# Two transformer blocks on one core: where the second block's modulation products run

## The chip, the cores and the metric

One NeuronCore of a Trainium2 chip runs the whole program. The metric is the device time of one execution in microseconds (us); the median of a few executions counts. TensorE (PE) multiplies matrices, VectorE (DVE), ScalarE (ACT) and GpSimd (POOL) work element by element, and SP does nothing here but issue transfers (DMA).

## What is computed

A first block mixes a sequence of 256 tokens, 1024 wide, with a diagonal state space model; a second model of two layers follows, whose norms and gates are modulated by a condition vector. Cut to what the change touches:

```python
def first_block(x, ...):                       # DEPTH = 1
    h = rmsnorm(x, norm_mix)
    x = x + s5_mixer(h, ...)                   # state space, then a * sigmoid(g), [a, g] = gelu(y) @ w_glu
    x = x + sqrelu_mlp(rmsnorm(x, norm_ffn), mlp_w1, mlp_w2)
    x = x + (p @ ple_w) * sigmoid(rmsnorm(x, norm_ple) @ ple_gate_w)
    return rmsnorm(x, norm_final)

def second_block(x, c, ctx, c_ctx, w_ada, b_ada, ...):
    for l in range(2):
        mod_x = silu(c) @ w_ada[l] + b_ada[l]      # (1, 6144): shift, scale, gate, twice
        mod_c = silu(c_ctx) @ w_ada[l] + b_ada[l]
        ...                                        # hx = modulate(rms_norm(x), ...), four mixers, swiglu
```

The modulation products are `silu(c) @ w_ada[l]` for two vectors at once: two columns against a matrix of 1024 x 6144 in float32, 25 MB of weights per layer. All of it is read once.

## The kernel before, in words

Activations lie features on partitions, 256 tokens along the free axis. Layer weights come by `wunits` (lines 340 to 351) in units of 128 x 1024: a transfer by SP, a cast on ACT to the high part `wh`, a subtraction on VectorE to the low part `wl`. `mm3` (353 to 365) then makes three matmuls for each 128 x 128 piece: high by high, high by low, low by high.

**Stages.** `s5` (655 to 808) is the state space stage. `s5_params` (496 to 596) computes decay powers on VectorE in many small operations. For eight groups of states `b_outer` makes outer products, which TensorE transposes and multiplies with the input (699 to 725). Then `c_outer` makes the output side (732 to 737) and `s5_scan` runs the scan on VectorE. TensorE forms Toeplitz blocks `kt` (742 to 757), which 32 transfers per run, 16 for each half, scatter into `mt` (759 to 763; the last of them on SP is kept as `m_dma`), and two sets of products with `mt` (780) and with the scanned states `zf` (792) give the output. `ple_proj` (826) loads and multiplies the side input; it is put behind `m_dma` on that transfer's queue (1707). `block1` (841) is the gated unit over eight output tiles (847 to 860) and the feed-forward stage in four parts (868 to 901). The second block's layers follow: `mixer`, `ffn` (1572).

**Modulation products, first layer.** `ada_steps(g)` (951 to 967), for three groups g of 2048 columns, is a generator. Each of 16 steps takes a chunk of 128 x 1024 (0.5 MB, one SP transfer into a stage buffer) and makes four products of 256 columns into the four 32-partition column groups of one PSUM tile; the stationary side is the activated condition vector `sc` (`silu_c`, 940). A float32 product stands in the trace as two matmuls. Two more steps copy the sums out and turn them by four transposes (`ada_turn`, 969). In `s5` the stage buffers are the three of pool `wa` (1688); after `s5` they are the three buffers `k4a`.

**Modulation products, second layer.** `ada_late` (977 to 1004) goes over 12 blocks of 512 columns. VectorE multiplies each chunk's rows by the condition's value and adds them up (lines 992 and 994, four operations a step, four steps a block), and TensorE adds the 128 partitions up with a stationary matrix of ones: two products of 512 columns a block, one per vector (998). Every second block is turned.

**Order.** The calls `ada_next(n)` (1010) pull n steps at a place in the program; after `s5_params` 4, then 2 for each of eight groups on the input side and 2 for each of eight on the output side, 2 for each output tile of the gated unit, 1 for each of eight units of the first two feed-forward parts. A planner orders each engine's instructions from their place in the program, their inputs and its own estimate of times; steps of the modulation inside `s5` get a place 50 instructions later (`ADA_OFF`). The order on each engine and each queue is fixed before the run, and each engine takes its list strictly in that order. `issue_after(ins)` puts what is made inside it behind `ins` on that engine's list, without a wait of its own.

Of the kernel before, what the change touches and what calls it, by code (L numbers as in the profile page):

```python
# [17 lines left out]
P = 128  # L18
# [260 lines left out]
class Net:  # L279
    def __init__(self, tc, aps, dbg=None):  # L280
        self.tc, self.nc, self.a, self.dbg = tc, tc.nc, aps, dbg or {}
        nc = self.nc
        self.V, self.S, self.G, self.T = nc.vector, nc.scalar, nc.gpsimd, nc.tensor
        self.n = 0
        self.ln = "m"


# [65 lines left out]
    def mm3(self, out, unit, act, ks, off=0, start=True, stop=True, cols=None):  # L353

        wh, wl = unit
        n = len(ks)
        for i, k in enumerate(ks):
            c = off + i * P
# [296 lines left out]
    def s5(self):  # L655
# [6 lines left out]
        with self.lane("a"):  # L662
            dm = self.k2([P, 16, 2, 16], F32, "dm")
        G.tensor_tensor(dm.rearrange("p a b c -> p a (b c)"), self.eye2.unsqueeze(1).to_broadcast([P, 16, 32]),
                        par("d").unsqueeze(2).to_broadcast([P, 16, 32]), op=ALU.mult)
        self.s5_params()
        self.silu_c()

# [3 lines left out]
        for h in range(2):  # L672
# [8 lines left out]
            u2.append(u)  # L681
        self.ada_next(4)
        y = self.rstd(pss, 32, 1.0 / D, EPS)
# [15 lines left out]
        for jp in range(4):  # L699
            ss_sb = self.k4([P, 2, 2, 2, 64], F32, "ss")  # L700
            for jj in range(2):
                pt = self.q4.tile([P, 4, 2, 8, 16], F32, tag="pt", name=self.nm("pt"))
                self.b_outer(pt, (jp * 2 + jj) * 4, bre, bim)
                self.ada_next(2)
                pmt = self.k4([P, 4, 2, P], F32, "pmt")
# [26 lines left out]
        for j in range(8):  # L732
            c = self.k4([P, 8, 8, 16], F32, "ca")
            for g0 in (0, 4):
                self.c_outer(c[:, g0 : g0 + 4], j * 8 + g0, c1, c2)
            self.ada_next(2)
            ca[j] = c
# [4 lines left out]
        for half in range(2):  # L742
# [16 lines left out]
            for i in range(16):  # L759
                r4, g4 = i // 4, i % 4  # L760
                dma = (G if half and i % 3 == 2 else nc.sync).dma_start(
                    mt[half][32 * r4 : 32 * r4 + 32, g4, :, 0 : P - 32 * r4],
                    kt[half][32 * g4 : 32 * g4 + 32, :, 32 * r4 : P])
                if half and i % 3 < 2:
                    self.m_dma = dma
# [6 lines left out]
        pss = {}  # L772
# [68 lines left out]
    def block1(self, ya, pe, early, fill):  # L841
# [5 lines left out]
        for f in range(KC):  # L847
# [9 lines left out]
            self.ssq_add(ssq, x[:, f], f, KC)  # L857
            self.ada_next(2)
            if f == 4:
# [8 lines left out]
        for part in range(4):  # L868
            ma = Act(self, KC, L, "m")
            for c in range(4):  # L870
# [7 lines left out]
                self.split(*ma.pair(c * 2), s)  # L878
                if part < 2:
                    self.ada_next()  # L880
                if part >= 1:
# [95 lines left out]
    def ada_late(self):  # L977


        V, S, T = self.V, self.S, self.T  # L980
        for b in range(12):
            if b % 2 == 0:
                ps = self.px([P, 512])
            acc = self.stage([P, 2, 512], F32, "ac")
            for k in range(0, KC, 2):
                st = self.stage([P, 2, 512], F32, "wa")
                self.nc.sync.dma_start(st.rearrange("p a b -> p (a b)"), self.a["w_ada1"][b * 4 + k // 2])
                for i in range(2):
                    for v in range(2):
# [3 lines left out]
                        else:  # L993
                            V.scalar_tensor_tensor(acc[:, v], st[:, i], c, acc[:, v], op0=ALU.mult, op1=ALU.add)  # L994
                yield
            for v in range(2):
                r = 64 * (b % 2) + 32 * v
                T.matmul(ps[r : r + 32, :], self.ones[:, 0:32], acc[:, v], start=True, stop=True)
            if b % 2:
                pt = self.ada_turn(ps).rearrange("p i (q s) c -> p i q s c", s=2)  # L1000
                for q in range(2):
                    c0 = (b - 1 + q) * 4
                    S.copy(self.mod[1][:, c0 : c0 + 4, :], pt[:, :, q, :, 0])
                yield

# [636 lines left out]
    def run(self):  # L1642
        tc, nc = self.tc, self.nc
        V, S, G = self.V, self.S, self.G
        with ExitStack() as st:
# [19 lines left out]
            with ExitStack() as s5s:  # L1665
# [21 lines left out]
                nc.sync.dma_start(self.s5v[:, 1200:], self.a["s5"][:, 1200:])  # L1687
                self.stage = lambda shape, dt, s: self.wa.tile(shape, dt, tag="wa", name=self.nm(s))
                self.ada_off = ADA_OFF
# [130 lines left out]
```

## Time and profile before

| | us |
|---|---|
| median of 3 runs | 1978.75 (1974.57 to 1979.27) |
| profiled execution | 1979.86 |
| its span, first to last instruction | 1978.1 |
| TensorE busy | 1890.7 (96%) |
| VectorE busy | 1525.5 (77%) |
| ScalarE busy | 932.4 (47%) |

Times in rows are counted from the span's start. Busy time says how long an engine had an instruction under way; neighbouring matmuls overlap, so the distance from one start to the next tells what a matmul costs in a row of them. The share of one engine in the chain of waits tells how much of the span it decided.

### The profile page before, as it was taken

To read this page: it belongs to the slowest core of one execution; us is meant where nothing else is said; L and a number is where in the kernel's file an instruction comes from. 1 tells how busy PE (TensorE), PEld (TensorE's weight loads), DVE (VectorE), ACT (ScalarE), POOL (GpSimd) and SP (SyncE) were. 2 spreads that over 40 slices of the span, in tenths; PEclk is the share of its full clock that TensorE was granted. 3 is DMA by queue.
4 is the path that set the end of the run, shared out by engine and by line. 5 is a ranking of instruction groups with operands and counts; after the bars stand their busy time and mean duration, and the time that the engine had idled before them with its cause. 6 is when DMAs were issued, how large, how long until landed. Compare 5 with 4: busy or idle time off the path is not lost.

```text
span 1978.1 us, 35512 instructions
## 1 busy us (share of the span) xinstructions
PE 1890.7 (96%) x13842; PEld 1676.3 (85%) x13842; DVE 1525.5 (77%) x3078; ACT 932.4 (47%) x1587; POOL 112.1 (6%) x130
## 2 busy tenths in 40 slices
PE   2879999999999999999999999999999999999997
PEld 1567899998799997799998777777997799989997
DVE  9853777799987789998788577665779997776665
ACT  2453545555655555654553222222556664544443
POOL 5410100000000011000000000000100000010000
PEclk9989999999999999999999999999999999999998
DMA  5686556664345654246555455453555235555663
GB/s 183 223 264 225 183 181 196 192 181 142 98 138 170 200 181 158 62 127 206 175 181 159 124 170 150 152 167 112 146 171 160 71 107 172 180 181 163 191 191 107
DMA packets 103192, 323.45 MB, mean 164 GB/s; under 512 B 16416, under 2 KB 18608, under 8 KB 102640
## 3 DMA queue, kind: packets, MB, share of 16 engines
q1 hardware_dynamic: 102256, 319.53, 52.1%
q8 instruction: 109, 1.79, 0.4%
q0 software_dynamic: 336, 1.44, 0.2%
q14 instruction: 59, 0.48, 0.1%
q10 hardware_dynamic: 432, 0.21, 0.0%
HBM read 317.47 MB, written 1.05 MB: 161 GB/s over the span
## 4 chain that ended last, share of the span: by engine, by line
PE 79%; DVE 12%; DMA 4%; ACT 2%; issue 2%; SPq 1%; POOL 0%; DVEq 0%; ACTq 0%; POOLq 0%
PE pm L363 19%; PE pm L364 19%; PE pm L365 18%; DVE wl L332 4%; PE pm L1071 3%; PE pm L1072 3%; PE pm L1073 3%; DVE cy L1102 2%; DMA wa<-w_ada 2%; PE px L960 2%; PE px L1393 2%; PE px L1342 1%; PE px L1375 1%; PE px L404 1%; ACT wh L331 1%
## 5 line engine op out<-in xcount | busy, mean ns | idle before, releaser
L331 ACT CAST wh<-ws 128x1024 fp32r<-128x1024 f32 (+3 forms) x556 | 533.1, 961 | 713.3 <-PE pm L364 403.6
L332 DVE TENSOR_TENSOR wl<-ws,wh 128x1024 fp32r<-128x1024 f32 (+3 forms) x556 | 616.1, 1116 | 270.7 <-ACT wh L331 267.7
L363 PE MATMUL pm<-h,wh 128*128 128x256 f32 (+1 forms) x928 | 297.8, 321 | 0.0
L364 PE MATMUL pm<-h,wh 128*128 128x256 f32 (+1 forms) x928 | 297.2, 320 | 0.0
L365 PE MATMUL pm<-h,wl 128*128 128x256 f32 (+1 forms) x928 | 296.8, 320 | 0.0
L363 PE MATMUL pm<-m,wh 128*128 128x256 f32 (+1 forms) x704 | 211.6, 301 | 0.0
L364 PE MATMUL pm<-m,wh 128*128 128x256 f32 (+1 forms) x704 | 211.2, 300 | 0.0
L365 PE MATMUL pm<-m,wl 128*128 128x256 f32 (+1 forms) x704 | 210.6, 300 | 0.0
L363 PEld LDWEIGHTS pm<-h,wh 128*128 128x128 f32 x928 | 174.6, 188 | 18.5 <-ACT wh L331 4.2
L364 PEld LDWEIGHTS pm<-h,wh 128*128 128x128 f32 x928 | 174.8, 188 | 14.6 <-issue 0.8
L365 PEld LDWEIGHTS pm<-h,wl 128*128 128x128 f32 x928 | 174.6, 188 | 14.4
L363 PE MATMUL pm<-hx,wh 128*128 128x256 f32 x640 | 183.3, 286 | 0.0
L364 PE MATMUL pm<-hx,wh 128*128 128x256 f32 x640 | 179.9, 281 | 0.0
L365 PE MATMUL pm<-hx,wl 128*128 128x256 f32 x640 | 179.6, 281 | 0.0
L1102 DVE SCALAR_TENSOR_TENSOR cy<-up,vecs,cy 128x256 f32<-128x256 f32 x360 | 161.9, 480 | 1.4
L363 PEld LDWEIGHTS pm<-m,wh 128*128 128x128 f32 x704 | 132.2, 188 | 9.3 <-ACT wh L331 1.7
L994 DVE SCALAR_TENSOR_TENSOR ac<-wa,sc,ac 128x512 f32<-128x512 f32 x168 | 117.8, 749 | 28.8 <-DMA wa<-w_ada 28.8
L364 PEld LDWEIGHTS pm<-m,wh 128*128 128x128 f32 x704 | 132.6, 188 | 7.5 <-issue 1.7
L365 PEld LDWEIGHTS pm<-m,wl 128*128 128x128 f32 x704 | 132.5, 188 | 5.7
L429 POOL TENSOR_TENSOR ssq<-ssq,sq 128x256 f32<-128x256 f32 x45 | 44.9, 999 | 1425.9 <-ACT sq L423 1424.4
L363 PEld LDWEIGHTS pm<-hx,wh 128*128 128x128 f32 x640 | 121.0, 189 | 2.2 <-issue 2.0
L365 PEld LDWEIGHTS pm<-hx,wl 128*128 128x128 f32 x640 | 121.0, 189 | 0.0
(444 smaller groups left out, 4224.0 us busy)
## 6 DMA issues: line engine op xcount, KB each, us to landing
wa<-w_ada SPq DMA_DIRECT2D x96, 512.0 KB, 4.1
ws<-w_gp SPq DMA_DIRECT2D x96, 512.0 KB, 3.6
ws<-w_f SPq DMA_DIRECT2D x88, 512.0 KB, 4.4
ws<-w_tok SPq DMA_DIRECT2D x76, 512.0 KB, 3.8
ws<-mlp_w SPq DMA_DIRECT2D x64, 512.0 KB, 4.2
ws<-w_gp SPq DMA_DIRECT2D x96, 256.0 KB, 2.7
ws<-w_f2a SPq DMA_DIRECT2D x32, 512.0 KB, 4.1
ws<-w_cin SPq DMA_DIRECT2D x24, 512.0 KB, 4.5
```

Of the source, the lines that this page charges most:

```text
L331: self.S.copy(hi, src)
L332: self.V.tensor_tensor(lo, src, hi.bitcast(F32), op=ALU.subtract)
L363: self.T.matmul(out, h, ah, start=start and i == 0, stop=False)
L364: self.T.matmul(out, h, al, start=False, stop=False)
L365: self.pe_last = self.T.matmul(out, l, ah, start=False, stop=stop and i == n - 1)
L429: (eng or self.G).tensor_tensor(acc, acc, sq, op=ALU.add)
L960: T.matmul(ps[32 * q : 32 * q + 32, hf * 256 : hf * 256 + 256], self.sc[:, k, :], st[:, q, :], start=k == 0, stop=k == KC - 1)
L994: V.scalar_tensor_tensor(acc[:, v], st[:, i], c, acc[:, v], op0=ALU.mult, op1=ALU.add)
L1071: self.T.matmul(ps, hi, a, start=k == 0, stop=False)
L1072: self.T.matmul(ps, lo, a, start=False, stop=False)
L1073: self.pe_last = self.T.matmul(ps, hi, b, start=False, stop=k == KC - 1)
L1102: V.scalar_tensor_tensor(y[:, k], up[:, k, i : i + L], w[:, i : i + 1], y[:, k], op0=ALU.mult, op1=ALU.add)
```

## The change

All 54 steps of the first layer's modulation are pulled inside `s5`: 6 ahead of `s5_params` (with the activation of the condition vector ahead of those), 3 in place of 2 for each group on the input and on the output side. The calls in the gated unit and in the first block's feed-forward stage go. Of the first 30 stage buffers two in five are halves of the residual `x`, which is loaded only later; so five are in turn instead of three. Of the second half's 16 scatter transfers, the 11 that SP issued are issued by ACT, so `m_dma` is ACT's. In the second layer a block's sums are made one step later than its last addition, as four products of 256 columns in four column groups, and the next `mm3` is put behind the last of them. All steps of the second layer then run in the first layer's `ffn`, 49 of them.

```diff
--- before.py
+++ after.py
@@ -283,6 +283,7 @@
         self.V, self.S, self.G, self.T = nc.vector, nc.scalar, nc.gpsimd, nc.tensor
         self.n = 0
         self.ln = "m"
+        self.ada_last = None
 
 
     def nm(self, s):
@@ -352,6 +353,10 @@
 
     def mm3(self, out, unit, act, ks, off=0, start=True, stop=True, cols=None):
 
+        if self.ada_last is not None:
+            was, self.ada_last = self.ada_last, None
+            with self.tc.issue_after(was.ins):
+                return self.mm3(out, unit, act, ks, off, start, stop, cols)
         wh, wl = unit
         n = len(ks)
         for i, k in enumerate(ks):
@@ -663,8 +668,9 @@
             dm = self.k2([P, 16, 2, 16], F32, "dm")
         G.tensor_tensor(dm.rearrange("p a b c -> p a (b c)"), self.eye2.unsqueeze(1).to_broadcast([P, 16, 32]),
                         par("d").unsqueeze(2).to_broadcast([P, 16, 32]), op=ALU.mult)
+        self.silu_c()
+        self.ada_next(6)
         self.s5_params()
-        self.silu_c()
 
         sh = [P, 32, 32]
         u2 = []
@@ -679,7 +685,6 @@
             u = self.k4(sh, F32, "u2")
             G.tensor_tensor(u, x2, par("gain")[:, h * 32 : h * 32 + 32].unsqueeze(2).to_broadcast(sh), op=ALU.mult)
             u2.append(u)
-        self.ada_next(4)
         y = self.rstd(pss, 32, 1.0 / D, EPS)
         for h in range(2):
             V.tensor_tensor(u2[h], u2[h], y.unsqueeze(1).to_broadcast(sh), op=ALU.mult)
@@ -701,7 +706,7 @@
             for jj in range(2):
                 pt = self.q4.tile([P, 4, 2, 8, 16], F32, tag="pt", name=self.nm("pt"))
                 self.b_outer(pt, (jp * 2 + jj) * 4, bre, bim)
-                self.ada_next(2)
+                self.ada_next(3)
                 pmt = self.k4([P, 4, 2, P], F32, "pmt")
                 for g2 in range(2):
                     ps = self.pm([P, 4, P])
@@ -733,7 +738,7 @@
             c = self.k4([P, 8, 8, 16], F32, "ca")
             for g0 in (0, 4):
                 self.c_outer(c[:, g0 : g0 + 4], j * 8 + g0, c1, c2)
-            self.ada_next(2)
+            self.ada_next(3)
             ca[j] = c
 
         zf = self.s5_scan(zb)
@@ -758,7 +763,7 @@
 
             for i in range(16):
                 r4, g4 = i // 4, i % 4
-                dma = (G if half and i % 3 == 2 else nc.sync).dma_start(
+                dma = (nc.scalar if half and i % 3 < 2 else G if half else nc.sync).dma_start(
                     mt[half][32 * r4 : 32 * r4 + 32, g4, :, 0 : P - 32 * r4],
                     kt[half][32 * g4 : 32 * g4 + 32, :, 32 * r4 : P])
                 if half and i % 3 < 2:
@@ -855,7 +860,6 @@
             V.scalar_tensor_tensor(x[:, f], s, 0.5, x[:, f], op0=ALU.mult, op1=ALU.add)
             self.split_scaled(ha.hi(f), ha.lo(f), x[:, f], self.vec("norm_ffn", f))
             self.ssq_add(ssq, x[:, f], f, KC)
-            self.ada_next(2)
             if f == 4:
                 nc.sync.dma_start(self.cx.rearrange("p a b -> p (a b)"), self.a["cT"])
         r2 = self.k1([P, L], F32, "r2")
@@ -876,8 +880,6 @@
                 S.activation(s, ps, AF.Relu)
                 V.tensor_tensor(s, s, s, op=ALU.mult)
                 self.split(*ma.pair(c * 2), s)
-                if part < 2:
-                    self.ada_next()
                 if part >= 1:
                     next(early, None)
             for c in range(4):
@@ -977,10 +979,26 @@
     def ada_late(self):
 
 
+
         V, S, T = self.V, self.S, self.T
+        pss = []
+
+        def products(b, acc):
+            if b % 2 == 0:
+                pss.append(self.px([P, 512]))
+            ps = pss[-1]
+            for q in range(2):
+                for v in range(2):
+                    r = 64 * q + 32 * v
+                    self.ada_last = T.matmul(ps[r : r + 32, b % 2 * 256 : b % 2 * 256 + 256], self.ones[:, 0:32],
+                                             acc[:, v, q * 256 : q * 256 + 256], start=True, stop=True)
+            if b % 2:
+                pt = self.ada_turn(ps).rearrange("p (b i) (q s) c -> p b q i s c", b=2, s=2)
+                for i in range(2):
+                    c0 = (b - 1 + i) * 4
+                    S.copy(self.mod[1][:, c0 : c0 + 4, :].rearrange("p (q i) s -> p q i s", i=2), pt[:, i, :, :, :, 0])
+
         for b in range(12):
-            if b % 2 == 0:
-                ps = self.px([P, 512])
             acc = self.stage([P, 2, 512], F32, "ac")
             for k in range(0, KC, 2):
                 st = self.stage([P, 2, 512], F32, "wa")
@@ -992,16 +1010,12 @@
                             V.tensor_scalar(acc[:, v], st[:, i], c, None, op0=ALU.mult)
                         else:
                             V.scalar_tensor_tensor(acc[:, v], st[:, i], c, acc[:, v], op0=ALU.mult, op1=ALU.add)
+                if k == 0 and b:
+                    products(b - 1, was)
                 yield
-            for v in range(2):
-                r = 64 * (b % 2) + 32 * v
-                T.matmul(ps[r : r + 32, :], self.ones[:, 0:32], acc[:, v], start=True, stop=True)
-            if b % 2:
-                pt = self.ada_turn(ps).rearrange("p i (q s) c -> p i q s c", s=2)
-                for q in range(2):
-                    c0 = (b - 1 + q) * 4
-                    S.copy(self.mod[1][:, c0 : c0 + 4, :], pt[:, :, q, :, 0])
-                yield
+            was = acc
+        products(11, was)
+        yield
 
     def ada_bias(self, l):
         b = self.vec("b_ada", l * 48, 48).unsqueeze(2).to_broadcast([P, 48, 2])
@@ -1685,7 +1699,16 @@
                 for h in range(2):
                     nc.sync.dma_start(self.x2[h].rearrange("p g c -> p (g c)"), self.a["x2"][:, h * 1024 : h * 1024 + 1024])
                 nc.sync.dma_start(self.s5v[:, 1200:], self.a["s5"][:, 1200:])
-                self.stage = lambda shape, dt, s: self.wa.tile(shape, dt, tag="wa", name=self.nm(s))
+                stages = iter(range(99))
+
+                def stage(shape, dt, s):
+                    i = next(stages)
+
+                    if i < 30 and i % 5 > 2:
+                        return self.x[:, i % 5 * 4 - 12 : i % 5 * 4 - 8]
+                    return self.wa.tile(shape, dt, tag="wa", name=self.nm(s))
+
+                self.stage = stage
                 self.ada_off = ADA_OFF
                 self.todo = chain(*(self.ada_steps(g) for g in range(3)))
                 ya = self.s5()
```

## Rows read from the trace of the kernel before

**Rows 1.** Chain that ended last, share of the span by engine.

```profile
PE 79%; DVE 12%; DMA 4%; ACT 2%; issue 2%; SPq 1%; POOL 0%; DVEq 0%; ACTq 0%; POOLq 0%
```

**Rows 2.** Windows by stage: stretch, length, busy per engine (instructions), clock, DMA share, GB/s.

```profile
4.00:17.00 13.00, 0.00 (x0) 0.00 (x0) 12.55 (x56) 0.41 (x2) 6.19 (x4) 1.00 0.86 326
17.00:32.00 15.00, 1.51 (x4) 0.63 (x4) 14.96 (x53) 5.31 (x11) 7.04 (x5) 1.00 0.00 0
32.00:74.00 42.00, 36.21 (x358) 18.68 (x359) 33.91 (x59) 20.65 (x43) 22.43 (x23) 0.96 0.63 205
74.00:104.00 30.00, 21.91 (x480) 13.58 (x484) 28.49 (x64) 11.68 (x36) 11.17 (x10) 0.94 0.87 255
104.00:123.00 19.00, 12.77 (x271) 10.82 (x269) 9.43 (x13) 6.32 (x7) 6.66 (x18) 0.73 0.77 182
135.60:209.79 74.19, 74.19 (x523) 53.67 (x521) 29.78 (x39) 26.57 (x41) 3.67 (x5) 1.00 0.72 243
213.00:241.00 28.00, 25.68 (x218) 24.88 (x218) 26.05 (x59) 17.30 (x31) 6.30 (x5) 1.00 0.61 182
1020.00:1410.00 390.00, 389.03 (x1868) 311.65 (x1866) 266.53 (x417) 114.59 (x169) 9.57 (x10) 1.00 0.48 148
```

**Rows 3.** Timeline of TensorE, gated-unit stage: start, us, engine, line, operation, out and in.

```profile
135.61 0.28 PE L363 MATMUL pm<-y,wh 128*128 128x256 f32 x1
...
140.93 0.28 PE L365 MATMUL pm<-y,wl 128*128 128x256 f32 x1
141.14 0.64 PE L960 MATMUL px<-wa,sc 128*32 128x256 f32 x8
...
142.02 0.62 PE L960 MATMUL px<-wa,sc 128*32 128x256 f32 x2
...
145.40 0.28 PE L365 MATMUL pm<-y,wl 128*128 128x256 f32 x1
...
209.79 0.39 PE L363 MATMUL pm<-h,wh 128*128 128x256 f32 x1
```

**Rows 4.** Waits, TensorE's (20 to 135 us) and SP's (30 to 105): total, times, longest.

```profile
PE px L960 <- POOL sc L949: 25.5, 1, 25.5
...
SPq L958 <- PE px L960: 56.6, 26, 19.4
```

**Rows 5.** Chunks and their products to 105 us: duration ns, first and last start.

```profile
L960 PE MATMUL px<-wa,sc x256: 379/403/637, 25.5 to 101.3; 128*32 128x256 f32 x128
...
DMA to landing us min/median/max: 3.2/4.5/10.9
```

**Rows 6.** Timeline of SP's queue from 0 to 134 us.

```profile
3.98 92.38 SPq L958 DMA_DIRECT2D wa<-w_ada  x32
96.44 19.67 SPq L761 DMA_DIRECT2D mt<-kt  x27
```

**Rows 7.** Toeplitz copies, state copies (duration ns, first and last start); VectorE's end of scan.

```profile
L757 ACT COPY kt<-px x4: 585/585/585, 82.1 to 104.8; 128x512 f32<-128x512 f32 x4
...
L632 ACT COPY zf<-zb x4: 1060/1080/1100, 105.5 to 108.8; 64x512 f32<-64x512 f32 x4
...
108.86 3.92 DVE L633 TENSOR_TENSOR zf<-t,t 64x480 f32<-64x480 f32 x4
```

**Rows 8.** Groups of instructions: busy us, mean ns; idle before, and releaser.

```profile
L994 DVE SCALAR_TENSOR_TENSOR ac<-wa,sc,ac 128x512 f32<-128x512 f32 x168 | 117.8, 749 | 28.8 <-DMA wa<-w_ada 28.8
```

**Rows 9.** Timeline of TensorE around two blocks' column sums, second block's feed-forward.

```profile
1124.80 0.40 PE L365 MATMUL pm<-h,wl 128*128 128x512 f32 x1
1125.13 1.05 PE L998 MATMUL px<-ac,ones 128*32 128x512 f32 x4
...
1126.45 0.39 PE L364 MATMUL pm<-m,wh 128*128 128x512 f32 x1
...
1142.78 0.39 PE L365 MATMUL pm<-m,wl 128*128 128x512 f32 x1
1143.10 1.05 PE L998 MATMUL px<-ac,ones 128*32 128x512 f32 x2
...
1145.81 0.40 PE L365 MATMUL pm<-m,wl 128*128 128x512 f32 x1
```

## The prediction

> **What bounds the kernel now.** I read the chain of waits first: 79% of the span is TensorE and 12% VectorE [rows 1]. So a microsecond is worth something only where TensorE is full, or where TensorE waits for the work that moves. Next I cut the span into stages and read busy time, clock and DMA rate of each [rows 2], then looked into each stage that the change touches. Four things are to be seen.
>
> In the gated-unit stage (135.6 to 209.8 us) TensorE runs without a gap, and modulation products stand between the layer's matmuls. Before the first of them, 47 steps of the layer's matmuls take 140.93 − 135.61 = 5.32 us, 0.113 us each. Then eight products run adjacent, and four pairs stand singly, each between two layer matmuls [rows 3].
>
> In the state space stage the transfer queue and TensorE hold each other up. The first product waits until 25.5 us for the activated condition vector, though its weights landed long before [rows 4]. The three stage buffers are full meanwhile, and DMA moves nothing from 17 to 32 us [rows 2]. From then on SP mostly waits for a product to free a buffer [rows 4]; the 32 chunks reach to 101.3 us [rows 5]. From 74 to 104 us VectorE is busy 28.49 of 30 us, from 32 to 74 only 33.91 of 42 [rows 2].
>
> The hand-over out of that stage is serial. The Toeplitz blocks are complete at 104.8 + 0.6 us, but SP issues the 27 scatter transfers after the last chunk, from 96.44 for 19.67 us, and all later loads queue behind them [rows 6, 7].
>
> In the first feed-forward stage of the second block (1020 to 1410 us) TensorE is busy 389 of 390 us [rows 2], so what its 24 column-sum products take is paid in full.
>
> **The gated-unit stage: −30 us.** Two of the 16 removed chunks fall to each of eight output tiles. From the layer matmul at 140.93 to that at 145.40 there are six steps of the layer's own; they would take 6 × 0.113 = 0.68 us and take 4.47, so the products cost 3.79 us per tile, 30.3 us for eight. As a check: 209.79 − 135.61 = 74.2 us hold 384 layer matmuls, 43.4 us; 30.8 are left, with some small sums in them [rows 3]. I take 30. No other engine steps in: in that stage VectorE has 29.78 us of work and ACT 26.57 [rows 2], almost none of it the products', and both fit in the 44 us that are left. What comes next is the load of the layer's weights, 1 MB per 5.4 us or some 190 GB/s, under the 243 of now [rows 2].
>
> **The first feed-forward stage of the first block: −2 us.** Three column-sum steps (12 VectorE operations of 0.75 us, 9 us) leave it [rows 8]. From 213 to 241 us VectorE is busy 26.05 of 28 us and TensorE lacks 2.3 us [rows 2]; I take 2 of these. The 9 us land in the second block's feed-forward stage, where VectorE has 390 − 267 = 123 us free. They cost nothing there as long as that idle time lies between the steps; without it they cost up to 9 us.
>
> **The column sums as four adjacent products: −7 us.** Today a group of four matmuls of 512 columns stretches two layer intervals (2 × 0.23 us, 512 columns taking twice the 0.113 of 256) to 1126.45 − 1124.80 = 1.65 us, so it costs 1.19; where a layer matmul stands between the pairs, three intervals take 1145.81 − 1142.78 = 3.03, a cost of 2.33 [rows 9]. Of the 12 blocks seven are of the first kind, three of the second, and two stand together at the stage's start, which I price like the first: 9 × 1.19 + 3 × 2.33 = 17.7 us. The new form, eight matmuls of 256 columns in four column groups, has a twin here: the eight adjacent first-block products at 141.14. From 140.93 to 142.02 there are 1.09 us where two layer intervals would take 0.23: 0.86 us [rows 3]. 12 × 0.86 = 10.3, a gain of 7. The bound on the other side is that the four don't overlap: two lone pairs cost 2.33 us [rows 9], so one product of 512 columns 1.17, one of 256 half of it, four in line 2.3 us, and 12 blocks 28 us, a loss of 10. The new edge makes the next layer product wait on TensorE until the four are issued; they read an accumulator finished one step before, some 8 us by 49 steps in 390 us, so I cost the wait at nothing. Cover gone, see the last rival.
>
> **The state space stage and hand-over: −6 us, between −14 and +11.** 16 chunks, with their SP issues, 128 matmuls and one more turn of the sums come in. TensorE pays 16 × 0.64 us [rows 3] of work; it lacks 8.1 us from 74 to 104 and is empty before 25.5 [rows 2, 4], so this is covered as long as weights are there. Weights decide: 48 chunks of 0.52 MB and 3.1 MB of other loads are 28.3 MB. At 326 GB/s, the rate from 4 to 17 us with many transfers under way, they take 87 us; at 255, the rate with three buffers from 74 to 104, 111 us [rows 2]. So the last product ends between 87 and 112 us, against 101.3: −14 to +11. Five buffers for 30 chunks is nearer to the first row, so I take some 92 us. But then VectorE is next: its scan chain ends at 112.8 us [rows 7], and can come forward only by what VectorE idles from 32 to 74 us, 8.1 us, part of which was TensorE waiting for chunks. I take 3 us of it.
>
> Moving the vector's activation ahead changes no work: its two small POOL operations pass POOL's product that waited for the parameters. The 11 transfers that leave SP for ACT shorten SP's list by 11 × 0.61 = 6.7 us [rows 6], and the next weight loads no longer stand behind them. On ACT they meet the four state copies from 105.5 on, 4.3 us [rows 7]: 105.4 + 6.7 + 4.3 = 116.4, about where SP's last issue now ends (116.1), so the scatter itself lands no earlier on their account; only the weights behind it do, of which I count 3 us. Queued behind them on ACT are the state copies and, after them, the casts of the next weights. That gives −6.
> The Trainium skill, "Trainium Kernel Development and Optimization", section Key Constraints, says that transfers issued from SP, ACT and POOL run on the same 16 DMA engines, and that several issuers save issue time alone. By it nothing beyond those 6.7 us could come from the move; a view of the queues as separate would have given the whole 10.7 us from 105.4 to 116.1.
>
> **Sum.** −30 − 2 − 7 − 6 = −45 us. The profiled execution took 1979.9 us for a span of 1978.1, 1.1 above the median of 1978.75; against the median that is 1934 us.
>
> **The rivals.**
> *DMA is the bound of the state space stage.* For it: SP already waits there on buffers, and the last 14 chunks run at 255 GB/s. Against it: 15 us without any transfer are filled. The blocks are then 11 us late instead of 6 early: 1934 + 17 = 1951. It decides if the chunk rate stays under 280 GB/s (28.3 MB in the 101 us of now).
> *The hand-over at the low clock.* From 104 to 123 us the granted clock is already 0.73, with TensorE waiting for transfers [rows 2]; 0.73 is a mix of the two levels, 1.2 and 2.4 GHz. With the products done earlier there is less work on TensorE before the block products, and they could run wholly at 1.2: 12.77 × 0.73 / 0.5 = 18.6 us, 5.9 more. That gives 1940.
> The Trainium skill, "TensorE: Matmul & The Clock Gate", Part 1, holds that the throttled state is the default and activity releases it. By that rule taking filler products out of this stretch speaks against the change; the trace agrees so far, with 1.00 in the full stages and 0.73 here.
> *The four products do not overlap, so the change does not do what it says.* Then −7 becomes +10: 1951. Against it stand the eight adjacent products of rows 3, in the same four column groups.
> *Slower: TensorE held behind late column sums.* The edge puts the next layer matmuls behind the products. Two accumulators now live at once, so of three stage buffers one is left for chunks at a block's start. If a block's sum is late by one chunk (4.5 us landing [rows 5]) and its four operations (3.0 us [rows 8]), 12 × 7.5 = 90 us are lost: 1934 + 90 = 2024. It decides from 45 / 12 = 3.8 us of waiting per block. For it: VectorE waited for chunks, 28.8 us in all [rows 8]. Against it: over 48 chunks that is 0.6 us each, and the sums have a step's lead.
>
> **How the numbers follow.** Forecast 0.62, DMA bound 0.22, low clock 0.08, no overlap 0.04, late sums 0.04. Low end: all sizes at their good bound, −31 − 2 − 9 − 14, about 1922. High end: 1951 and 6 us less gain in the two TensorE terms, 1957. About 0.3% (6 us) is what a measurement can tell from no change. All cases but the last lie 27 us or more below the median; allowing some for sizes missed together, faster 0.93, same 0.03, slower 0.04.
>
> **What would show it.** Right: no product line between the layer's matmuls of the gated-unit stage, and that stage near 44 us; chunks under way without a pause from 4 us, the 48th product before 101 us; column-sum groups that cost under 1 us each. Wrong: products ending after 110 us with TensorE waiting for chunks (rival one); a clock near 0.5 in the hand-over (two); groups of 2 us (three); TensorE idle before each group (four). The forecast as a whole is wrong if the gated-unit stage stays above 55 us, or if the first layer matmul comes more than 15 us later than 135.6.

## The result and the profile after

The changed kernel takes 1952.17 us (median of four runs, 1949.74 to 1956.21) against 1976.66 us of the kernel before (four runs). The ratio is 0.9876, 95% interval 0.9857 to 0.9894: 24.5 us faster. The forecast was 45 us faster, 1934; the time lies in its range of 1922 to 1957, but not for the reason forecast: one term missed by 28.6 us, more than the 23 between the forecast and the high end, and by luck other terms came some 10 us larger than forecast. The profiled execution took 1949.74 us for a span of 1948.0, 2.4 under its median. So the two traces differ by 30.1 us, 5.6 more than the medians.

Four places in both traces divide the difference. All columns are us; the state space stage is taken to the first layer matmul of the gated unit, and the third row reaches to the end of the first layer's mixer in the second block.

| stretch | before | after | change | forecast |
|---|---|---|---|---|
| start to first gated-unit matmul | 135.61 | 158.17 | +22.6 | -6 |
| gated-unit stage | 74.18 | 44.80 | -29.4 | -30 |
| first block's feed-forward to mixer | 823.1 | 815.9 | -7.3 | -2 |
| feed-forward with the column sums | 400.5 | 388.4 | -12.1 | -7 |
| the rest | 544.7 | 540.8 | -3.9 | 0 |

Every term of the forecast but one came as large as forecast, within 1 us, or larger. The state space stage came out 28.6 us worse than forecast. Whether the rest belongs to the change is not shown: all kernels with the new column sums take 540.2 to 543.2 us for it, experiment 1 below, which has them alone, 540.2, and of the kernel without them there is one trace. The changed kernel's windows, counterpart of [rows 2] (columns as there):

```profile
4.00:17.00 13.00, 3.03 (x24) 0.63 (x24) 12.55 (x56) 0.42 (x2) 6.38 (x5) 1.00 1.00 389
17.00:38.00 21.00, 5.34 (x34) 1.90 (x30) 20.86 (x65) 9.48 (x15) 11.97 (x9) 1.00 0.35 136
52.00:80.00 28.00, 28.00 (x217) 13.19 (x216) 16.29 (x25) 13.12 (x31) 12.07 (x13) 1.00 0.54 178
86.00:104.00 18.00, 15.36 (x370) 9.63 (x362) 17.15 (x26) 7.01 (x20) 7.54 (x7) 1.00 0.84 286
104.00:130.00 26.00, 11.56 (x140) 3.70 (x136) 15.57 (x44) 5.48 (x6) 3.09 (x5) 0.66 0.93 263
158.17:202.97 44.80, 44.64 (x395) 44.44 (x393) 31.73 (x39) 25.68 (x40) 5.03 (x5) 1.00 0.66 201
1018.83:1407.18 388.35, 386.98 (x1952) 316.80 (x1951) 272.51 (x426) 116.48 (x172) 9.74 (x10) 1.00 0.50 152
```

The weights start as hoped, 389 GB/s from 4 to 17 us, then fall to 136 from 17 to 38 us. From 52 to 80 us TensorE is busy all 28.00 us while the DMA engines are at 0.54. From 104 to 130 us it is the other way: TensorE has 11.56 of 26 us and the DMA engines are at 0.93. So no single engine bounds the stage; the limit changes hands twice. TensorE's timeline shows the first two (a product in f32 is two instructions, so x2 is one product and x8 the four of a chunk).

```profile
18.67 1.08 PE L962 MATMUL px<-x,sc 128*32 128x256 f32 x8 [0.18 <-DMA x<-w_ada]
31.49 0.64 PE L684 MATMUL px<-sm,cst 128*128 128x32 f32 x2 [11.74 <-DVE sm L683]
34.71 0.64 PE L684 MATMUL px<-sm,cst 128*128 128x32 f32 x2 [2.58 <-DVE sm L683]
36.89 1.08 PE L962 MATMUL px<-wa,sc 128*32 128x256 f32 x8
...
67.20 0.62 PE L962 MATMUL px<-wa,sc 128*32 128x256 f32 x2
67.75 0.33 PE L715 MATMUL pm<-ident,pt 128*128 128x128 f32 x1
68.01 0.62 PE L962 MATMUL px<-wa,sc 128*32 128x256 f32 x2
68.56 0.33 PE L715 MATMUL pm<-ident,pt 128*128 128x128 f32 x1
...
128.29 1.08 PE L962 MATMUL px<-wa,sc 128*32 128x256 f32 x8 [1.24 <-DMA wa<-w_ada]
130.08 1.11 PE L976 MATMUL px<-ident,adas 128*128 128x128 f32 x4 [0.71 <-ACT adas L973]
134.66 4.78 PE L785 MATMUL py<-mt,u 128*32 128x128 f32 x61 [3.46 <-DMA mt<-kt]
...
141.12 0.32 PE L785 MATMUL pm<-mt,u 128*32 128x128 f32 x3
```

Five chunks are done by 19.75 us; the sixth, though its step is pulled ahead of `s5_params`, comes at 36.89. In TensorE's program its products stand behind two products that need sums from VectorE (L684) and the first two transposes (L715), and VectorE, busy with the parameters, delivers these late. Until then the five buffers are full and SP issues no chunk; from 23 to 37 us the DMA engines move 32 GB/s. Later a chunk's four products no longer stand together; each stands between two transposes, 0.81 us from one to the next (67.20 to 68.01). Adjacent, all four cost 0.86 [rows 3]. The last product ends at 129.4 us, before at 101.7.

Behind it the hand-over is again serial. The two queues, SP's and then ACT's:

```profile
86.33 37.45 SPq L960 DMA_DIRECT2D wa<-w_ada  x18
123.86 15.51 SPq L766 DMA_DIRECT2D mt<-kt  x16
139.49 0.53 SPq L834 DMA_DIRECT2D pt<-pT  x1
```

```profile
94.70 0.59 ACT L762 COPY kt<-px 128x512 f32<-128x512 f32 x1
...
110.51 0.59 ACT L762 COPY kt<-px 128x512 f32<-128x512 f32 x1 [7.65 <-PE px L760]
111.13 3.26 ACTq L766 DMA_DIRECT2D mt<-kt  x4
114.49 4.37 ACT L637 COPY zf<-zb 64x512 f32<-64x512 f32 x4 [3.39 <-DMA mt<-kt]
118.90 0.61 ACTq L766 DMA_DIRECT2D mt<-kt  x1
129.44 0.59 ACT L973 COPY adas<-px 128x512 f32<-128x512 f32 x1 [10.59 <-PE px L962]
129.45 0.59 ACTq L766 DMA_DIRECT2D mt<-kt  x1
131.24 3.24 ACTq L766 DMA_DIRECT2D mt<-kt  x5
```

The first half's 16 scatter transfers stand behind the last chunk on SP (123.86), and half of ACT's stand behind the copy of the last group's sums, which waits 10.59 us for the last product. Before, the same transfers went out from 96.44 us on [rows 6].

By the trace, what stands behind the chunks turns their lateness into that of the stage. The first half's blocks are complete with the copy at 94.70 us, its transfers then wait 28.6 us, until 123.86, behind the last chunks on SP's list, and the products that read them (`pm<-mt,u`) start at 141.12. TensorE's list, too, has the products with `mt` behind those of the last chunk. All four block copies are done at 111.1 us, only 5.7 later than before, yet the gated unit starts 22.6 later. No instruction of the gated unit reads the modulation sums; the feed-forward stage behind it is the first to use them.

The waits from 0 to 160 us (total, times, longest; counterpart of [rows 4]) say the same: the wait for the condition vector is gone, and waits for weights have its place, 15.8 us beside the 13.7 of the first chunk.

```profile
PE px L962 <- DMA wa<-w_ada: 29.5, 15, 13.7
SPq L960 <- PE px L962: 69.4, 38, 17.8
```

The column sums, on TensorE's timeline (counterpart of [rows 9]): from 1115.26 to 1116.50 there are 1.24 us where two layer intervals take 0.46, so a group costs 0.78.

```profile
1115.26 0.40 PE L370 MATMUL pm<-m,wl 128*128 128x512 f32 x1
1115.59 0.64 PE L993 MATMUL px<-ac,ones 128*32 128x256 f32 x8
1116.16 0.51 PE L368 MATMUL pm<-m,wh 128*128 128x512 f32 x1
1116.50 0.39 PE L369 MATMUL pm<-m,wh 128*128 128x512 f32 x1
```

### The profile page after: what moved, and what is told of

Same layout as the page of the kernel before. It is cut to its first block, busy times and chain, and to the rows that moved or that the text cites. A ratio compares the mean times of both kernels' runs of the same rounds, so it can differ in the third digit from the quotient of the medians.

```text
span 1948.0 us, 35584 instructions
## 1 busy us (share of the span) xinstructions
PE 1863.6 (96%) x13890; PEld 1665.2 (85%) x13890; DVE 1527.9 (78%) x3078; ACT 932.2 (48%) x1587; POOL 112.3 (6%) x130
## 3 DMA queue, kind: packets, MB, share of 16 engines
q1 hardware_dynamic: 99936, 318.61, 52.5%
## 4 chain that ended last, share of the span: by engine, by line
PE 80%; DVE 12%; DMA 4%; issue 2%; ACT 2%; SPq 0%; DVEq 0%; ACTq 0%
PE pm L368 20%; PE pm L369 19%; PE pm L370 19%; DVE wl L333 4%; PE pm L1085 2%; PE pm L1087 2%; PE pm L1086 2%; DVE cy L1116 2%; DMA wa<-w_ada 2%; PE px L1407 2%; PE px L1356 1%; PE px L962 1%; PE px L1389 1%; PE px L409 1%; PE pm L378 1%
## 5 line engine op out<-in xcount | busy, mean ns | idle before, releaser
L434 POOL TENSOR_TENSOR ssq<-ssq,sq 128x256 f32<-128x256 f32 x45 | 44.3, 984 | 1366.3 <-ACT sq L428 1364.9
```

What stands on the lines that cost most here:

```text
L434: (eng or self.G).tensor_tensor(acc, acc, sq, op=ALU.add)
```

## The experiments

Theories before the first run: weight supply makes the state space stage late (main); TensorE's lone products between transposes do (rival); the scatter's queues do (second rival). All times below are medians, and "glu" is the first layer matmul of the gated unit in the profiled run. It varies by some 3 us from run to run: the kernel of the first experiment, whose state space stage is that of the kernel before, has it at 138.44 instead of 135.61.

**1. The column sums alone.** The kernel before with the new `ada_late` and the edge in `mm3`.

> The kernel before with the column-sum part of the change alone (four products of 256 columns in four column groups, and the edge behind them). If the change's gain outside the state space stage and the gated-unit stage is the column sums' own, the second block's first feed-forward stage gets 11 to 12 us shorter, as it did in the changed kernel, and the time is about 1977 - 11 = 1966 us. If the terms of the forecast hold, 7 us: 1970. If the four products did not overlap: 1987. If the shorter stage came from the three sums that no longer run in the first block or from other work that moved, under 4 us of gain is seen here: 1973 or more.

1968.22 us, ratio 0.9947 (0.9932 to 0.9963). The stretch with the sums takes 388.6 us instead of 400.5, so the whole gain of 12 us there is the sums' own. In all thirteen kernels with the new sums, the changed one among them, that stretch takes 387.6 to 390.2 us.

**2. The third group back in the gated unit**, all else as changed.

```diff
-        self.ada_next(6)
+        self.ada_next(4)
...
-                self.ada_next(3)
+                self.ada_next(2)
```

> The changed kernel with the third group of modulation products back in the gated-unit stage (32 chunks in the state space stage, as in the kernel before); the early activation, the five buffers, the queues of the scatter and the column sums stay as changed. If the 16 extra chunks are what makes the state space stage late (main theory), the last product of the stage ends before 105 us, the first layer matmul of the gated-unit stage comes at 125 to 137 us instead of 158, that stage is back at about 74 us, and the time is about 1952 - 24 + 29 = 1957, give or take 5. If the early start, the buffers or the moved scatter transfers are what makes the stage late, the first layer matmul stays beyond 150 us and the time is about 1980.

1967.01 us, ratio 0.9938 (0.9919 to 0.9957). The last product ends at 90.3 us, 11 earlier than before, and the blocks are complete at 100.0 instead of 105.4. Yet glu is at 138.7, outside the expected 125 to 137, and the time is outside the expected 1952 to 1962. The added chunks make 19.5 of the 22.6 us, and what the early start gained is gone again. ACT's timeline shows where it goes:

```profile
99.46 0.58 ACT L762 COPY kt<-px 128x512 f32<-128x512 f32 x1 [4.30 <-PE px L760]
100.08 2.94 ACTq L766 DMA_DIRECT2D mt<-kt  x4
105.54 1.10 ACT L637 COPY zf<-zb 64x512 f32<-64x512 f32 x1 [5.49 <-DVE zb L624]
105.63 0.61 ACTq L766 DMA_DIRECT2D mt<-kt  x1
...
109.25 2.21 ACTq L766 DMA_DIRECT2D mt<-kt  x3
```

After four issues ACT reaches the state copies, which wait until 105.54 us for VectorE's scan; the other seven issues stand behind and between them. The second half's products wait for the scatter until 118.4.

**3. Without the last 18 transfers.** Their products read a chunk that is there already.

```diff
+                if (g * 2 + hf) * 8 + k < 30:
                     self.nc.sync.dma_start(st..., self.a["w_ada0"][...])
```

> The changed kernel without the transfers of the last 18 of the 48 weight chunks: their products run on a chunk that is already there, so the first layer's modulation is computed from wrong weights in part. All matmuls, copies and other transfers stay. If the weight transfers bound the state space stage (main theory), the last product ends before 110 us instead of 129, the first layer matmul comes at 133 to 143 us instead of 158, and the time is 1927 to 1937. If TensorE bounds it (product pairs that stand singly between transposes from 52 to 80 us), the input side still ends at 82 us and less than 5 us are gained: 1947 or more. If it is the scatter behind the chunks on SP's queue alone, SP is free at about 86 us, and the gain is the same as by the main theory, so a second run with the scatter moved off SP has to tell these two apart.

1940.98 us in one run; last product 102.8, glu 140.5. Without the late transfers 17.7 of the 22.6 us are gone. But the input side (its last transposes) still ends at 84.7 us (before: 74.3), and the blocks are complete at 110.9, no earlier than in the changed kernel. That part is not the transfers'. Whether the 17.7 us are the late weights' alone is open: SP's first scatter transfer goes out at 104.14 us here instead of 123.86. As the expectation says, this run can't tell the two apart, and no run put the scatter ahead of the chunks.

**4. Third group in the gated unit, four products adjacent**, on the kernel of experiment 1.

```diff
+                if not self.ada_off:
+                    self.ada_last = m
```

> The kernel before with the new column sums, and with the 16 chunks of the third group left in the gated-unit stage, where the next layer matmul now waits on TensorE until a chunk's four products are issued, so that these stand adjacent. If what the 16 chunks cost in that stage is that their products stand singly (a lone pair costs 1.17 us, four adjacent products 0.43), each chunk costs 0.43 instead of 1.9 us: 23 us less there, and with 11 us of the column sums 1977 - 34 = 1943 us, under the changed kernel. If the edge makes the layer matmuls wait for the chunks' landing, the stage stays at 70 us or more, with TensorE idle ahead of the products, and the time is 1962 or more.

1952.61 us, ratio 0.9871 (0.9841 to 0.99): as fast as the whole change, with nothing moved. The gated-unit stage takes 57.7 us, so a chunk costs (57.7 - 44.8) / 16 = 0.81 us instead of 1.9, not the 0.43 expected. TensorE waits for a chunk only once (0.9 us); two chunks together cost 1.2 us by the timeline (143.99 to 145.42 less two intervals of 0.115).

**5 and 6. Two remedies for the supply**, each on the changed kernel: 14 chunks' products ordered ahead of the parameters' first product and transposes; five buffers for all 48 chunks.

```diff
-        self.ada_next(6)
+        self.ada_next(14)
+        ahead = self.ada_m
...
+            with self.tc.issue_after(ahead.ins):
                 T.matmul(pss, self.blk16, ss, ...)
```

> The changed kernel with 14 chunks' products ahead of the first product and the first transposes that wait for the parameters (6 now), so that TensorE frees the stage buffers, and weights are under way, from 20 to 38 us, where DMA now stands still; three chunks per group on the input side, two on the output side. If that pause is what the stage is short of (main theory: 18 us at some 2 us a chunk are 8 or 9 chunks), the last product ends at 110 to 117 us instead of 129, the first layer matmul comes at 141 to 148 us instead of 158, and the time is 1935 to 1942. If the product pairs that stand singly between transposes bound the stage, the input side still ends near 82 us, the last product comes after 122 us, and the time stays above 1945. If the pause is only moved to a later place, no more than 3 us are gained.

> The changed kernel with five stage buffers for all 48 chunks (in the changed kernel the last 18 have three), and nothing else. If the three buffers are what holds the last 18 chunks to some 263 GB/s, their rate from 86 us on goes to 300 GB/s or more, 9.4 MB take 31 us or less instead of 36, the last product ends 5 us or more earlier (124 us or less), and the time is about 1947. If the rate there is not set by the buffers but by the packets and the other transfers, the last product stays within 2 us of 129 and the time near 1952.

Fourteen ahead: 1942.71 us in one run; last product 121.5, glu 151.2: a little short of the first case, while the input side ends at 85.5 us, no earlier than without the edit (82.6), as in the second. The pause is filled, and the next limit stands in the windows:

```profile
17.00:38.00 21.00, 13.92 (x98) 3.58 (x95) 20.69 (x63) 9.48 (x15) 12.12 (x10) 1.00 0.93 361
52.00:80.00 28.00, 27.87 (x235) 13.89 (x228) 12.63 (x19) 12.35 (x26) 8.68 (x9) 0.91 0.52 167
```

361 GB/s instead of 136, but from 52 to 80 us still 167 with TensorE full. Five buffers: 1949.71 us in one run, last product 126.1, glu 156.3, between the two cases. From 86 to 104 us 333 GB/s instead of 286, then 239: hardly a gain, and within the spread of single runs.

**7. Experiment 2 with the scatter back on SP's queue and the third group's products adjacent.**

```diff
-                dma = (nc.scalar if half and i % 3 < 2 else G if half else nc.sync).dma_start(
+                dma = (G if half and i % 3 == 2 else nc.sync).dma_start(
```

> The kernel with the third group back in the gated-unit stage (1967 us), with two edits: its 11 scatter transfers that went to ACT's queue are back on SP's as in the kernel before, and a layer matmul follows a chunk's four products, so that these stand adjacent. If the issues on ACT held up the hand-over (there they stood behind the state copies, which wait for VectorE's scan until 105 us), the first layer matmul comes at 128 to 134 us instead of 138.7; with the gated-unit stage at 58 us instead of 74 that makes 1967 - 16 - 7 = 1944, from 1940 to 1948. If the landing of the scatter and not its issue sets the hand-over, the first layer matmul stays at 137 us or later and the time is 1950 or more.

1942.71 us, ratio 0.9824 (0.9797 to 0.985); glu 128.1 instead of 138.7, though the last block copy starts only 1.0 us earlier. Some 9 us are the queue's: SP issues all 27 in one piece. The gated-unit stage takes 62.1 us, not the 58 expected; TensorE waits 3.4 us for chunks there.

```profile
88.29 20.01 SPq L766 DMA_DIRECT2D mt<-kt  x27
```

So with 32 chunks the early start and five buffers are worth 7.5 us (128.1 against 135.6; 10.3 against the 138.4 of experiment 1), and the scatter on ACT took all of it.

**8. Three remedies together** on the changed kernel: experiments 5 and 6, and the scatter on SP.

> All three remedies for the changed kernel's state space stage at once: 14 chunks' products ahead of the parameters, five stage buffers for all 48 chunks, and the scatter on SP's and POOL's queues as in the kernel before. If chunk supply is what made the stage late, all 48 products end by 100 to 108 us, the first layer matmul comes at 132 to 140 us and the time is 1952 - 18 to 1952 - 26, that is 1926 to 1934. If TensorE's single pairs bound it, the last product ends after 115 us and the time is 1940 or more.

1935.59 us, ratio 0.9795 (0.9769 to 0.9822); last product 111.2, glu 143.2. Between the two cases: from 52 to 80 us TensorE is busy 27.85 of 28 us, and the input side still ends at 84.2.

**9. The same with the transposes behind the products**, so that no product stands alone on the input side.

```diff
-                        with self.tc.issue_after(ahead.ins):
+                        with self.tc.issue_after(self.ada_m.ins):
                             T.transpose(ps[:, i, :], pt[:, g4, ri]..., self.ident)
```

> The kernel with the three remedies (1935.6 us) with one edit: on the input side of the state space stage each group's transposes come after the chunks' products that were taken before them, so that a chunk's four products stand adjacent and no pair stands alone. If TensorE's single pairs are what now holds the input side (27.85 of 28 us busy from 52 to 80, a pair with the transpose behind it 0.81 us), some 15 chunks cost 0.5 instead of 1.6 us each, the input side ends 6 us or more before 84 us, the first layer matmul comes at 135 to 139 us instead of 143, and the time is about 1930. If the chunks' landing bounds it, TensorE waits for weights ahead of the transposes, the input side ends no earlier, and the time is 1935 or more.

1927.42 us, ratio 0.9752 (0.9727 to 0.9777), the fastest of all: some 25 us under the changed kernel. The input side ends at 78.9 us (5.3 earlier, where 6 or more were expected), the last product at 96.8, glu is at 133.2, 10 us from one ordering edge. Its windows and two lines of its TensorE timeline:

```profile
17.00:38.00 21.00, 16.18 (x118) 4.15 (x111) 20.69 (x63) 10.07 (x16) 12.11 (x10) 1.00 0.95 368
52.00:80.00 28.00, 26.73 (x338) 15.80 (x330) 18.51 (x28) 15.69 (x38) 14.68 (x15) 1.00 0.89 314
```

```profile
62.17 1.07 PE L965 MATMUL px<-wa,sc 128*32 128x256 f32 x16
63.17 1.09 PE L718 MATMUL pm<-ident,pt 128*128 128x128 f32 x8
```

From 52 to 80 us TensorE does 338 matmuls where it did 217 in the changed kernel, in 26.73 us instead of 28.00, and the weights come at 314 GB/s instead of 178: two chunks in a row take 1.00 us (62.17 to 63.17), one lone product with its transpose 0.81. The Trainium skill, "TensorEngine Tiling (Array Packing)", section Tiling Modes under Key Properties, has a rule for it: a change of tiling mode, not of the tile, drains TensorE. The trace agrees as to the price: a product with a stationary side of 32 columns, alone between two of 128, has 0.55 us to itself, in a row of eight 0.125 (1.00 / 8). That a drain is what the time goes into, no row shows.

**10. Forty chunks in the state space stage**, eight in the gated unit, on the kernel of experiment 8.

> The kernel with the three remedies (1935.6 us) with 40 chunks in the state space stage and the last eight in the gated-unit stage, one per output tile, each with its four products adjacent. If the cost of a chunk in the state space stage rises with their number (143.2 us for the first layer matmul with 48 against 128.1 with 32: 0.94 us a chunk) and one alone per tile costs 0.5 to 0.6 us in the gated-unit stage, the first layer matmul comes at about 136 us, the gated-unit stage takes 49 us, and the time is 1932 to 1934. If the stage's transfers are the price wherever the chunks stand (two per tile cost 1.1 us each in the gated-unit stage), nothing is gained: 1935 to 1938.

1934.9 us, ratio 0.9799 (0.9767 to 0.9831): no gain. glu comes at 132.5, 10.7 earlier, but the gated-unit stage takes 52.5 us instead of 44.3. One chunk alone among the layer's matmuls costs 0.77 us on TensorE (138.03 to 139.03 less two intervals), not 0.5 to 0.6, and 6.2 of the 8.2 us are that.

**11 and 12. One remedy on the changed kernel**: transposes behind products alone, then the scatter on SP as well.

> The changed kernel (1952 us) with one edit: on the input side of the state space stage each group's transposes come after the chunks' products taken before them. Six chunks' products ahead of the parameters, three buffers for the last 18 chunks and the scatter's queues stay as changed. If single pairs were the larger part of the lateness (10 us of it, as the last two kernels differ), the input side ends at 75 instead of 82 us, the last product comes before 119 us, the first layer matmul at 146 to 150 us instead of 158, and the time is about 1942. If chunk supply alone was the cause, TensorE waits for weights in front of the transposes instead, the first layer matmul stays within 3 us of 158, and the time is 1949 or more.

> The kernel of the run before with the scatter back on SP's and POOL's queues. If the scatter on ACT still costs here what it cost with 32 chunks (about 9 us of the 10.6 between 138.7 and 128.1), because half of its issues stand behind the copy of the last group's sums, which waits for the last product, the first layer matmul comes 5 to 9 us earlier than without this edit. If with 48 chunks SP is busy with chunks until the end anyway, all 27 issues follow the last chunk there, and the first layer matmul moves by less than 3 us. What is then left to the 133.2 us of the kernel with all edits is the pause and the buffers.

1946.94 us (ratio 0.9851, 0.9837 to 0.9866) and 1943.87 us (0.9842, 0.9825 to 0.9858). Alone the order gives glu 151.2, less than expected for it: from 52 to 80 us weights now come at 299 GB/s, but from 17 to 38 us still at 135, and 18 chunks are still loaded over three buffers, from 73.8 to 113.5 us. The scatter on SP moves glu by 0.4 us here, as the second case had it: SP is busy with chunks until 111 us anyway (the medians differ by 3.1 us, but their intervals overlap). What is left from there to experiment 9, 150.8 to 133.2, is the pause and the buffers; no run separates these two once the products stand together.

## Why the prediction was right and wrong

**Gated-unit stage, -30: right.** 29.4 us, with no product line left between the layer's matmuls, and the stage at 44.8 (44 forecast).

**First block, -2: undersized.** The stretch from its feed-forward stage to the mixer lost 7.3 us. Kernels that leave the third group in the gated unit and the first block (the one before, experiments 1, 2, 4 and 7) take 822 to 828 us for it, all that move it whole 814 to 818. The step that failed is "I take 2 of these": it read 28 us of the stage for a stretch of over 800. By the first layer matmul of the stage's second part (282.96 us before, 271.49 after) 4.6 us are gained: TensorE idles 0.25 us up to there instead of 2.3, which is the 2 that I took. What the rest of the 7.3 is was not traced.

**Column sums, -7: right in kind, undersized.** The ten new groups that stand alone cost 0.66 to 0.78 us, 0.86 forecast; all twelve, with the two at the stage's start, 9.9 instead of 18.6 us, by the intervals around each. That is 8.7 of the 12.1 us. TensorE idles 1.4 us in that stretch instead of 2.6; the remaining 2.2 I could not put down to single rows.

**State space stage, -6 within -14 and +11: wrong, +22.6.** The step that failed is "Weights decide", and behind it "this is covered as long as weights are there". I let five buffers mean many transfers under way, and took rates from stretches. What frees a buffer is a product, and a product runs where it stands in TensorE's program. The sixth chunk stands there behind what waits for VectorE, so the empty stretch of 15 us in [rows 2] was not filled but moved: 32 GB/s from 23 to 37 us. And the extra products went between the transposes one at a time, at the price that I had read for the gated unit (lone products in [rows 3]) and not applied here: from 52 to 80 us TensorE is full and the transfers wait. The bound of +11 left both out. Experiments 5 and 11 take one of the two away and bring glu forward by 7 us each; experiment 9 shows that with both gone (and five buffers, and the scatter on SP) the stage is 25 us shorter, more than the sum. My reading is that while one remains, the other's stretch is only waited for elsewhere; what the buffers add once both are gone is not separated. That supply comes late at all counts because the scatter, and the products that read it, stand behind the chunks; how much it would count with these ahead stays untested.

**Hand-over, part of that -6: wrong in sign.** I counted 3 us of gain for the shorter list on SP. (My 0.61 us an issue is the trace's median for a single one; the 27 of [rows 6] take 0.73 each with the gaps between them.) Of the copies ahead of the 11 issues on ACT I priced the 4.3 us that they work, not what they wait for: VectorE's scan with 32 chunks (9 us, experiments 2 and 7), the last product with 48. With 48 chunks it hardly matters which of the two queues has the second half (0.4 us, experiment 12), because the chunks are late on SP too. The rule that I cited of the Trainium skill, "Trainium Kernel Development and Optimization", Key Constraints, that several issuers only save issue time, was not put to the test: no gain came. The loss is in no sentence of it.

**The rivals.** *DMA bounds the stage* is the one that came nearest: its sign, products after 110 us with TensorE waiting for chunks, is there (129.4 us; 15.8 us of waits), and its condition, a rate under 280 GB/s, is met from 17 to 86 and from 104 to 130 us. But its mechanism holds only in the second of these: from 52 to 80 us the DMA engines are at 0.54 and it is TensorE that is full. Its 1951 us agree with 1952 by two errors that offset each other: it allowed 17 us where 28.6 came, and took the small terms, 10 us too little, as the forecast did. Experiment 3 puts 17.7 of the 22.6 us on the late transfers and the scatter behind them; the input side's delay remained without them. *Low clock*: its sign is there, but before had it too. From 104 to 130 us 0.66 was granted, where TensorE waits and is not the bound; from 86 to 104 us, where most of the block products run, it was 1.00, the higher level. But 61 of the products with `mt` ran at 0.53, close to the lower level, and took 0.078 us each (4.78 us from 134.66 on); before, 56 of them took 0.072 each at 0.61. So little of the 22.6 us is the clock's. The window of each, the kernel before first, and its products:

```profile
104.80:116.26 11.46, 5.70 (x64) 4.55 (x65) 7.82 (x10) 4.90 (x5) 3.10 (x5) 0.61 0.72 141
112.63 4.05 PE L780 MATMUL pm<-mt,u 128*32 128x128 f32 x56 [2.37 <-DMA mt<-kt]
```

```profile
134.60:140.00 5.40, 5.29 (x84) 4.63 (x85) 0.00 (x0) 0.00 (x0) 0.00 (x0) 0.53 0.57 95
```

*No overlap* and *late sums* are out: groups at 0.78 us, none behind an idle TensorE.

By its own test, the first layer matmul more than 15 us after 135.6, the forecast as a whole was wrong. What it aimed at can be had, though not by this change: experiment 9 puts the scatter back on SP, pulls 14 chunks early instead of 6, orders TensorE's products and adds two buffers, and has all 48 products done by 96.8 us (some 92 forecast) and 1927 us.

## What to carry to other kernels

Before work is poured into another stage's gaps, look at where its instructions will stand in the engine's program: a gap in time is only usable by what stands ahead of the instruction that waits. Small column-group products among full-array matmuls should be kept together, by an explicit order where the scheduler spreads them. And a transfer issued by a compute engine waits for every copy that stands ahead of it there, so look for what those copies wait for. The same goes for a pure transfer queue: here the scatter that the next stage needed stood behind loads that it did not need.

## What the runs showed of the hardware

The DMA engines were busy 0.93 at 263 GB/s (104 to 130 us) and 1.00 at 389 (4 to 17 us) in the same trace: with the scatter among the weights, busy engines carried over a quarter less (263 / 0.93 = 283). That may be why five buffers gained so little in experiment 6 (0.90 at 239 GB/s there). No run isolates the cause: neither the scatter's short rows nor anything else that differs between the two stretches.
